# Fixed U columns as three 256-wide products, two more places for look-up operands, and counted gate rows one per step

## The chip, the cores and the metric

The kernel runs on one core of a Trainium2 chip. The metric is the device time of one execution in microseconds (us). TensorE multiplies matrices, VectorE and ScalarE work on rows, GpSimd does some row work and issues the DMAs whose rows are picked by index, SyncE's queue issues the plain loads. In the profile these are PE (PEld is its weight load), DVE, ACT, POOL and SP.

## The reference

One layer over 256 tokens of width 2048: retention and an RG-LRU side by side, cross attention over 256 memory tokens, then PEER, and a last norm. The change is in PEER:

```python
def peer_ffn(xn, w_q, sub_keys, u_tab, v_tab):
    q = (xt @ w_q).reshape(t, PEER_HEADS, 2, PEER_HALF)
    sub_scores = jnp.einsum('thcd,hckd->thck', q, sub_keys)
    vals, ids = lax.top_k(sub_scores, PEER_TOPK)
    cand = vals[:, :, 0, :, None] + vals[:, :, 1, None, :]
    top_sc, pos = lax.top_k(cand.reshape(t, PEER_HEADS, 256), PEER_TOPK)
    ...
    eid = (i1 * PEER_N_KEYS + i2)              # (t, 128) of 16384 experts
    gate = jax.nn.softmax(top_sc, axis=-1)
    ...
        act = gelu(einsum('td,tkd->tk', xb, u_tab[eid]))
        out = einsum('tk,tkd->td', gb * act, v_tab[eid])
```

All of it is float32.

## The kernel before

The 16384 experts are seen as 128 rows of 128. For 40 of these rows (`RD`), all 128 experts are computed for all 256 tokens, in five chunks of 8 rows: these are the fixed U columns and, later, chunks 0 to 4 of V. Of the other 88 rows' experts, the 32 groups that most tokens chose are gathered by a list (`dyn`, found by counting): four more chunks, 5 to 8, the gathered U and V columns. What is left over of a token's choices is taken token by token: 38 gathers of U for each half of the tokens (a dot product on VectorE, L1438) and 38 of V (an addition, L1446). All gathers are issued by GpSimd (L1431, L1215, L1263).

A product is kept exact to float32 by a split: the weights `raw` (128x1024, 512 KB) become `hi`, rounded on ScalarE (L133), and `lo`, the rest, on VectorE (L134); the activations `xn` stand as two halves of 256 columns, high and low. For a U column, `w_mms` (L136) does, for each of two halves of the weights, 8 products of `hi` with both halves of `xn` at once (512 wide, L143) and 8 of `lo` with the high half (256 wide, L145). Then `u_chunk` folds: ScalarE copies the right 256 columns of the sum (L1161), VectorE adds the left ones (L1162), ScalarE takes the gelu (L1163).

Beside the fixed U columns runs side work, in this order: `route` (the top-16 search, VectorE; for each half of the tokens it ends with three transposes `rT`, L835), `gbuild` (counting: for four tokens at a time, one-hot rows on VectorE, L1113, a product with the gates on GpSimd, L1114, gate products G and counts on TensorE, L1127 and L1130, copies on ScalarE, L1133 and L1134; after every 32 tokens ScalarE's queue writes the gates to DRAM, `gd` and `gt`, L1137 to L1140), then `side`: `choose` finds the 32 groups, and `look_up` marks for each token's choices whether their group was chosen. A look-up takes eight operands of 1 MB, loaded by `at_load` on GpSimd (L977) into four places: the tile of `h[1]` and three tiles `at1` to `at3`, which stand where gate tiles `gs` stood that the writes to DRAM still read. After that come `pick` (a max search), a sum over tokens (`off`, L1030) and the spilling of what does not fit (L1057, `fl` L1536). How the columns and the side work are mixed is set by a credit (`wv.pump` after each half column) and then by the scheduler, which orders each engine's queue; the order of the later part is written out (`run`).

`run` works through a list of steps: W (a plain tile of weights), D and R (halves of a gathered row of U and V), G (a tile of gates). At each step it splits the weights for step t+2 and issues loads for up to step t+8 into free places: `spots` for W and G (four `raw` tiles, and two halves of a `kept` tile, `lent`, in the V chunks), `rows_u`, and `rows_v` (L1342). The V chunks are taken in the order 0, 1, 2, 3, 5, 6, 7, 8, 4. The counted gates of chunks 5 to 8 are read back by `gate_rows` (L1290): four gathers of 128x256 in a row into one place of `spots`, twice for each chunk, during the V chunks 0 to 3. `gate_columns` (L1299) then multiplies four columns of the activations.

Of the kernel before, what the change touches and what calls it, by code (L numbers as in the profile page):

```python
# [9 lines left out]
F32 = mybir.dt.float32  # L10
F32R = mybir.dt.float32r
BF16 = mybir.dt.bfloat16
# [6 lines left out]
P = 128  # L19
# [66 lines left out]
def hybrid_layer_kernel(ctx: ExitStack, tc: tile.TileContext, a: dict, out: bass.AP, dbg=None):  # L86
# [50 lines left out]
    def w_mms(j, hi, lo, xt, pt):  # L137
        highs = [(0, 8 * j + k) for k in range(8)]
        lows = [(1, 8 * j + k) for k in range(8)]
        for part, kb in highs + lows if j == 0 else highs[:7] + lows + highs[7:]:  # L140
            ks = slice((kb - 8 * j) * P, (kb - 8 * j + 1) * P)
            if part == 0:
                PE.matmul(pt, hi[:, ks], xt[:, kb, :], start=(kb == 0), stop=(kb == KB - 1))  # L143
            else:
                PE.matmul(pt[:, :T], lo[:, ks], xt[:, kb, :T], start=False, stop=False)  # L145

    def whalf(j, src, xt, pt, raw=None):
        hi, lo = split(raw_tile(src) if raw is None else raw)
# [825 lines left out]

    def at_load(i):
        tt, c = divmod(i, 4)
        G.dma_start(ats[i % 4].bitcast(BF16), i1d[tt, 32 * c:32 * c + 32].rearrange("s t -> (s t)")[None, :].to_broadcast([P, 32 * P]))  # L977

    def look_up(tt):
        fl = gx["b"][:, 1920:2048]  # L980
# [23 lines left out]
    def compact():  # L1004
# [68 lines left out]
                                   op0=ALU.is_equal, op1=ALU.mult, accum_out=spl["g"][:, bs])  # L1073
            yield 0.6
        count_rest()
        ring.extend(ats[1:])

    tr = {}

    def side():  # L1080
        tr["t"] = rp.tile([P, P + 1], F32, tag="cand", name="tri")
        nc.sync.dma_start(tr["t"], a["tri"])
        wv.rate = RK
        for i in (1, 2, 3):
            ats.append(slot("ms", [P, D], f"at{i}"))
            at_load(i)
        yield from choose()
        yield from compact()
# [65 lines left out]
    def u_chunk(i, cols=8):  # L1154
        new_act(i)
        for c in range(cols):
            pt = mm("U") if i or c else pt0
            if i or c:
                wblock([a["U"][8 * i + c, j] for j in range(2)], xn, pt)
            t = tp.tile([P, T], F32, tag="fold", name="foldu", bufs=1)  # L1160
            A.copy(t, pt[:, T:])  # L1161
            V.tensor_tensor(t, pt[:, :T], t, op=ALU.add)  # L1162
            A.activation(acts[i][:, c, :], t, AF.Gelu_apprx_tanh)  # L1163

    acc = {}

# [116 lines left out]
    def prep_steps(i, gap=2):  # L1283
        box = []

        def gate(g, tt):
            av = acts[i][:, :, tt * P:(tt + 1) * P].rearrange("p c (b t) -> p c b t", t=GT)
            V.tensor_tensor(av, g.rearrange("p (b c t) -> p c b t", c=8, t=GT), av, op=ALU.mult)

        def gate_rows(b, q):  # L1290
            for n in range(4):
                k = 8 * (i - NCH) + 4 * q + n
                G.indirect_dma_start(b[:, T * n:T * n + T], None, gt_,
                                     bass.IndirectOffsetOnAxis(ap=dyn[:, k:k + 1], axis=0),
                                     bounds_check=NS - 1, oob_is_err=False)

        def gate_columns(g, q):
            av = acts[i][:, 4 * q:4 * q + 4]
            V.tensor_tensor(av, g.rearrange("p (c t) -> p c t", c=4), av, op=ALU.mult)  # L1299
# [12 lines left out]

        reads = []
        if ND <= i < NCH:
            n = T // GT // TT
            reads = [Step("G", lambda b, tt=tt: nc.sync.dma_start(
                b, gd[i - ND, :, n * tt:n * tt + n].rearrange("p b c t -> p (b c t)")),
                lambda g, tt=tt: gate(g, tt), 0) for tt in range(TT)]
        elif i >= NCH:
            reads = [Step("G", lambda b, q=q: gate_rows(b, q), lambda g, q=q: gate_columns(g, q), 0)  # L1320
                     for q in range(2)]
        post = {1: [(lambda: rounded(0), None)], 1 + gap: [(lambda: rounded(1), lambda: left(0))],
                1 + 2 * gap: [(None, lambda: left(1))]}
        return reads, {} if i in PLAIN else post
# [5 lines left out]
    ahs, spare = {}, {}  # L1330
    spots, rows_u, rows_v, lent = [], [], [], []

    def run(steps):
        raws, his, los, pts, later = {}, {}, {}, {}, {}
        queues = {k: [t for t, s in enumerate(steps) if s.kind in k and s.load] for k in ("WG", "D", "R")}
        free = {"WG": spots, "D": rows_u, "R": rows_v}

        def loads(t):
            for k, q in queues.items():
                while q and q[0] <= t + (4 if k == "R" else 0) and free[k]:  # L1340
                    t = q.pop(0)
                    raws[t] = free[k].pop(0)  # L1342
                    if k != "WG":
                        raws[t + 1] = raws[t]
                    steps[t].load(raws[t])

# [8 lines left out]
                    rows_u.append(raws[t])  # L1355

        def high(t):
            if t < len(steps) and steps[t].kind != "G" and not steps[t].plain:
                his[t] = ws.tile([P, 1024], F32R, tag="hi", name="hi", bufs=4)
                if steps[t].kind == "D":  # L1360
                    for n in range(2):
                        A.copy(his[t][:, 512 * n:512 * n + 512], pts[t][n])  # L1362
                else:
                    A.copy(his[t], part_of(t))  # L1364
# [4 lines left out]
        def low(t):  # L1369
            if t >= len(steps) or steps[t].plain:  # L1370
                return
            kind = steps[t].kind
            if kind == "G":
                steps[t].mms(raws[t])
            else:
                los[t] = ws.tile([P, 1024], F32R, tag="lo", name="lo", bufs=3)
# [6 lines left out]
                    V.tensor_tensor(los[t], part_of(t), his[t].bitcast(F32), op=ALU.subtract)  # L1383
            if kind in "WG":
                spots.append(raws[t])
            elif kind == "R" and steps[t].part:
# [15 lines left out]
        for t, step in enumerate(steps):  # L1402
# [5 lines left out]
            high(t + 3)  # L1408
            low(t + 2)
            loads(t + 8)  # L1410
            if step.plain:
                step.mms(raws[t])
                if step.part:
                    rows_v.append(raws[t])
                del raws[t]
            elif step.kind != "G":
# [6 lines left out]
            if step.kind != "G":  # L1423
# [252 lines left out]
    while "xn" not in done:  # L1676
        wv.pump(1.0)
    pt0 = mm("U")
    wblock([a["U"][0, 0], a["U"][0, 1]], xn, pt0)
    for b in (KB - 2, KB - 1):  # L1680
        sub_scores(b)
    pa.__exit__(None, None, None)
# [69 lines left out]
    for n, (i, nxt) in enumerate(zip(ORDER[:-1], ORDER[1:])):  # L1752
# [7 lines left out]
                attach(part[-1], {1: [(lambda m=m: given(m), None)]})  # L1760
        for k, g in enumerate(reads if nxt < NCH else []):
            part.insert(2 + 5 * k, g)
        if n < len(early_reads):
            for k, g in enumerate(early_reads[n]):
                part.insert(12 + 3 * k, g)
        steps += part
    with tc.manual_schedule(engines=ENGINES):
        run(steps)
# [95 lines left out]
```

## Time and profile before

| | |
|---|---|
| median of three runs | 2024.96 us |
| the three runs | 2024.9, 2024.96, 2029.99 us |
| the profiled execution | 2025.13 us, its span 2023.3 us |
| mean granted clock of TensorE | 0.974 |
| PE, DVE, ACT, POOL busy | 1897.9, 1518.9, 863.6, 508.4 us |
| HBM read, written | 503.24 MB, 21.30 MB (259 GB/s over the span) |
| U loads, V loads, to landing (median) | 3.8 us, 8.5 us |

The span is from the first to the last instruction of the profiled execution. Busy times of matmuls have modelled ends, so products that follow each other overlap in them; how close they follow is read from their starts. A wait is put down to what ended last before it. The fixed U columns run from 875 to 1259 us of the span, the gathered ones to 1514, the V chunks to 1952.

### The profile page before, as it was taken

To read this page: it belongs to the slowest core of one execution; us is meant where nothing else is said; L and a number is where in the kernel's file an instruction comes from. 1 tells how busy PE (TensorE), PEld (TensorE's weight loads), DVE (VectorE), ACT (ScalarE), POOL (GpSimd) and SP (SyncE) were. 2 spreads that over 40 slices of the span, in tenths; PEclk is the share of its full clock that TensorE was granted. 3 is DMA by queue.
4 is the path that set the end of the run, shared out by engine and by line. 5 is a ranking of instruction groups with operands and counts; after the bars stand their busy time and mean duration, and the time that the engine had idled before them with its cause. 6 is when DMAs were issued, how large, how long until landed. Compare 5 with 4: busy or idle time off the path is not lost.

```text
span 2023.3 us, 27282 instructions
## 1 busy us (share of the span) xinstructions
PE 1897.9 (94%) x10004; PEld 1556.1 (77%) x10004; DVE 1518.9 (75%) x2348; ACT 863.6 (43%) x1364; POOL 508.4 (25%) x371
## 2 busy tenths in 40 slices
PE   9999999999999999999898779999899799989798
PEld 8888888888889888888788767889787577455463
DVE  6868967754566557999978657899798797666667
ACT  6566444544555455554456523333343333020211
POOL 1200010000000000000045410555436556466524
PEclk9999999999999999999999889999899899999999
DMA  8775656566655457556458694998989799979983
GB/s 295 260 228 171 201 178 193 162 192 194 183 175 156 144 180 296 171 168 208 150 142 163 158 297 142 397 403 289 381 319 378 275 365 397 349 286 380 388 342 123
DMA packets 203242, 499.84 MB, mean 247 GB/s; under 512 B 106760, under 2 KB 113032, under 8 KB 174856
## 3 DMA queue, kind: packets, MB, share of 16 engines
q1 hardware_dynamic: 72288, 254.23, 38.0%
q0 software_dynamic: 36240, 228.29, 29.0%
q10 hardware_dynamic: 94576, 15.54, 4.4%
q8 instruction: 79, 1.29, 0.3%
q14 instruction: 59, 0.48, 0.1%
HBM read 503.24 MB, written 21.30 MB: 259 GB/s over the span
## 4 chain that ended last, share of the span: by engine, by line
PE 55%; DMA 15%; DVE 11%; issue 10%; POOL 5%; ACT 2%; ACTq 1%; POOLq 0%; SPq 0%; DVEq 0%
PE wb L143 10%; PE xc L185 6%; PE xc L186 6%; PE xc L188 6%; PE wb L145 5%; PE U L143 5%; DMA at<-in_Us_dram,idx 4%; PE acc L1613 3%; DVE lo L134 3%; PE U L145 2%; DMA gt<-gs 2%; DMA raw<-in_V_dram 2%; POOL at L1431 2%; DMA kept<-in_Vs_dram,dyn 1%; PE G L1127 1%
## 5 line engine op out<-in xcount | busy, mean ns | idle before, releaser
L134 DVE TENSOR_TENSOR lo<-raw,hi 128x1024 fp32r<-128x1024 f32 x364 | 448.7, 1235 | 206.9 <-PE xc L188 123.8
L133 ACT CAST hi<-raw 128x1024 fp32r<-128x1024 f32 x364 | 381.8, 1052 | 287.0 <-PE xc L186 173.0
L143 PE MATMUL U<-xn,hi 128*128 128x512 f32 x1152 | 314.3, 409 | 0.0
L143 PEld LDWEIGHTS U<-xn,hi 128*128 128x128 f32 x1152 | 213.6, 195 | 36.8
L1438 DVE SCALAR_TENSOR_TENSOR junk<-at,h 128x2048 bf16<-128x2048 f32 x72 | 164.6, 2286 | 21.2 <-DMA at<-in_Us_dram,idx 21.1
L145 PEld LDWEIGHTS U<-xn,lo 128*128 128x128 f32 x1152 | 157.9, 192 | 23.5 <-DVE lo L134 12.3
L145 PE MATMUL U<-xn,lo 128*128 128x256 f32 x1152 | 163.2, 284 | 9.3 <-DVE lo L134 9.3
L1446 DVE SCALAR_TENSOR_TENSOR hh<-at,coef,hh 128x2048 f32<-128x2048 f32 x49 | 116.0, 2368 | 50.1 <-DMA at<-in_Vs_dram,idx 49.4
L1364 ACT CAST hi<-kept 128x1024 fp32r<-128x1024 f32 x52 | 53.9, 1051 | 198.7 <-DMA kept<-in_Vs_dram,dyn 111.2
L781 POOL DMA_DIRECT2D hn<-h x2 | 1.1, 565 | 509.0 <-DVE h L779 509.0
L143 PE MATMUL wb<-hT,hi 128*128 128x512 f32 x448 | 116.9, 396 | 0.0
L1431 POOL DMA_INDIRECT at<-in_Us_dram,idx x72 | 82.4, 1144 | 125.2 <-DVE junk L1438 102.0
L1197 PE MATMUL acc<-kept,kept 128*128 128x512 f32 x256 | 110.2, 592 | 0.0
L1114 POOL TENSOR_TENSOR kept<-kept 128x512 f32<-128x512 bf16 x64 | 77.5, 1218 | 122.9 <-DVE kept L1113 88.9
L1197 PEld LDWEIGHTS acc<-kept,kept 128*128 128x128 f32 x256 | 48.6, 190 | 60.5 <-issue 60.0
L143 PEld LDWEIGHTS wb<-hT,hi 128*128 128x128 f32 x448 | 80.6, 189 | 13.9
L1113 DVE TENSOR_TENSOR kept<-kept,kept 128x512 bf16<-128x512 bf16 x128 | 69.7, 591 | 28.0 <-POOL kept L1114 15.0
L1127 PE MATMUL G<-kept,kept 128*128 128x128 f32 x512 | 73.1, 295 | 18.5 <-POOL kept L1114 9.6
L1431 POOL DMA_INDIRECT at<-in_Vs_dram,idx x49 | 73.4, 1498 | 66.3 <-DVE hh L1446 28.8
L143 PE MATMUL wb<-xT,hi 128*128 128x512 f32 x352 | 88.9, 393 | 0.0
L1127 PEld LDWEIGHTS G<-kept,kept 128*128 128x128 f32 x512 | 67.2, 207 | 22.4 <-POOL kept L1114 13.1
L1380 DVE TENSOR_TENSOR lo<-uT,hi 128x512 fp32r<-128x512 f32 x128 | 82.0, 684 | 2.4 <-ACT hi L1362 1.4
(492 smaller groups left out, 4133.2 us busy)
## 6 DMA issues: line engine op xcount, KB each, us to landing
raw<-in_U_dram SPq DMA_DIRECT2D x80, 512.0 KB, 3.8
raw<-in_w_qkv_dram SPq DMA_DIRECT2D x48, 512.0 KB, 4.2
raw<-in_w_xyg_dram SPq DMA_DIRECT2D x44, 512.0 KB, 4.1
raw<-in_V_dram SPq DMA_DIRECT2D x44, 512.0 KB, 8.5
raw<-in_w_xk_dram SPq DMA_DIRECT2D x32, 512.0 KB, 3.6
raw<-in_w_xv_dram SPq DMA_DIRECT2D x32, 512.0 KB, 3.5
raw<-in_w_out_dram SPq DMA_DIRECT2D x32, 512.0 KB, 3.5
raw<-in_w_xq_dram SPq DMA_DIRECT2D x32, 512.0 KB, 3.5
```

The costliest lines, as they stand in the source:

```text
L133: A.copy(hi, raw)
L134: V.tensor_tensor(lo, raw, hi.bitcast(F32), op=ALU.subtract)
L143: PE.matmul(pt, hi[:, ks], xt[:, kb, :], start=(kb == 0), stop=(kb == KB - 1))
L145: PE.matmul(pt[:, :T], lo[:, ks], xt[:, kb, :T], start=False, stop=False)
L185: PE.matmul(pt, xh, hi[:, w], start=(n == 0 and k == 0), stop=False)
L186: PE.matmul(pt, xl, hi[:, w], start=False, stop=False)
L188: PE.matmul(pt, xh, lo[:, w], start=False, stop=(n == 7 and k == 1))
L1127: PE.matmul(pt.rearrange("p (c t) -> p c t", t=4)[:, :, j], o1[:, j], og[:, j], start=True, stop=True)
L1197: PE.matmul(acc[dc][tt], av[:, c, tt * P:(tt + 1) * P], row[:, dc * 512:(dc + 1) * 512], start=False, stop=False)
L1431: G.indirect_dma_start(dst, None, src, bass.IndirectOffsetOnAxis(ap=ix, axis=0), bounds_check=n - 1, oob_is_err=False)
L1438: V.scalar_tensor_tensor(junk, gat, 1.0, h[0], op0=ALU.mult, op1=ALU.mult, accum_out=coef[tt][:, k:k + 1])
L1446: V.scalar_tensor_tensor(hh[tt], gat, coef[tt][:, k:k + 1], hh[tt], op0=ALU.mult, op1=ALU.add)
```

## The change

1. The fixed U columns use `u_block`: for each half of the weights, 8 products of `hi` with the high half of `xn`, 8 of `hi` with its low half, and 8 of `lo` with the high half, all 256 wide and all into the same 256 columns. The gelu reads the sum directly; the copy and the addition are gone. The gathered U columns stay as they were.
2. Look-up operands have six places: `gx["a"]` and `gx["d"]`, which counting used for its one-hot rows, come after `at1` to `at3`, and five loads are issued at the start of `side`. Afterwards only the three `at` tiles go to the token gathers.
3. The counted gates of chunks 5 to 8 are read by a step of a new kind, K, which takes a whole row buffer of `rows_v` (2048 wide) instead of two places of `spots`. Its load puts eight gathers on a list, `pending`, and `run` issues one of them at each step, up to 12 steps ahead. One `gate_columns` multiplies all eight columns. The four K steps stand in V chunks 1, 2 and 3 of the order (one, two and one); before, two G steps stood in each of 0 to 3.

```diff
+    def u_block(srcs, pt):
+        for j, src in enumerate(srcs):
+            hi, lo = split(raw_tile(src))
+            for part in range(3):
+                for k in range(8):
+                    kb = 8 * j + k
+                    x = xn[:, kb, T:] if part == 1 else xn[:, kb, :T]
+                    PE.matmul(pt[:, :T], (lo if part == 2 else hi)[:, k * P:(k + 1) * P], x,
+                              start=(part == 0 and kb == 0), stop=(part == 2 and kb == KB - 1))
+            wv.pump(wv.rate)
...
-                wblock([a["U"][8 * i + c, j] for j in range(2)], xn, pt)
-            t = tp.tile([P, T], F32, tag="fold", name="foldu", bufs=1)
-            A.copy(t, pt[:, T:])
-            V.tensor_tensor(t, pt[:, :T], t, op=ALU.add)
-            A.activation(acts[i][:, c, :], t, AF.Gelu_apprx_tanh)
+                u_block([a["U"][8 * i + c, j] for j in range(2)], pt)
+            A.activation(acts[i][:, c, :], pt[:, :T], AF.Gelu_apprx_tanh)
...
-        G.dma_start(ats[i % 4].bitcast(BF16), ...)
+        G.dma_start(ats[i % 6].bitcast(BF16), ...)
...
-        for i in (1, 2, 3):
-            ats.append(slot("ms", [P, D], f"at{i}"))
+        ats.extend(slot("ms", [P, D], f"at{i}") for i in (1, 2, 3))
+        ats.extend((gx["a"], gx["d"]))
+        for i in range(1, 6):
             at_load(i)
...
-            reads = [Step("G", lambda b, q=q: gate_rows(b, q), lambda g, q=q: gate_columns(g, q), 0)
-                     for q in range(2)]
+            reads = [Step("K", lambda b: pending.extend((b, n, gate_row) for n in range(8)), gate_columns, 0)]
...
             loads(t + 8)
+            if pending:
+                b, n, f = pending.pop(0)
+                f(b, n)
...
-        if n < len(early_reads):
-            for k, g in enumerate(early_reads[n]):
-                part.insert(12 + 3 * k, g)
+        for m, k in ((0, 12),) if n == 1 else ((1, 6), (2, 15)) if n == 2 else ((3, 8),) if n == 3 else ():
+            part.insert(k, early_reads[m][0])
```

GpSimd's queue at the end of counting and the look-up, before (L1114 is counting's product, `i1d` the operands, `h` and `at` their places, `row` a gathered U column):

```order
L977 DMA at_10568<-i1d 128x4096
L1114 TENSOR_TENSOR kept_7748<-kept_7750 128x512 x2
L977 DMA h_4236<-i1d 128x4096
L977 DMA at_10566<-i1d 128x4096
L977 DMA at_10568<-i1d 128x4096
L977 DMA at_10570<-i1d 128x4096
L1215 DMA row_11592<-in_Us_dram,dyn 128x2048
L1215 DMA row_11593<-in_Us_dram,dyn 128x2048
L977 DMA at_10570<-i1d 128x4096
```

and now (`kept` are the two new places):

```order
L988 DMA at_10952<-i1d 128x4096
L1126 TENSOR_TENSOR kept_7764<-kept_7766 128x512 x2
L988 DMA kept_7766<-i1d 128x4096
L988 DMA kept_7763<-i1d 128x4096
L988 DMA h_4236<-i1d 128x4096
L988 DMA at_10951<-i1d 128x4096
L1224 DMA row_12112<-in_Us_dram,dyn 128x2048
L988 DMA at_10953<-i1d 128x4096
L1224 DMA row_12113<-in_Us_dram,dyn 128x2048
```

Loads 4 and 5 now stand ahead of the second use of `h` and `at1`; the load into the third place (`at_10953`), of operand 3, is the last one, and no load stands behind it.

TensorE's queue at the end of the side work, from a spill product to the first gathered column (`uT`), before:

```order
L1057 MATMUL spill<-ct,own 128x1 x2
L1536 MATMUL fl<-flag,ones 128x2
L143 MATMUL U<-xn,hi 128x512
L145 MATMUL U<-xn,lo 128x256 x8
L143 MATMUL U<-xn,hi 128x512 x9
L145 MATMUL U<-xn,lo 128x256 x8
L143 MATMUL U<-xn,hi 128x512 x7
L145 MATMUL U<-xn,lo 128x256 x8
L143 MATMUL U<-xn,hi 128x512 x9
L145 MATMUL U<-xn,lo 128x256 x8
L143 MATMUL U<-xn,hi 128x512 x7
L145 MATMUL U<-xn,lo 128x256 x8
```

and now:

```order
L1068 MATMUL spill<-ct,own 128x1 x2
L1548 MATMUL fl<-flag,ones 128x2
L154 MATMUL U<-xn,hi 128x256 x5
L154 MATMUL U<-xn,lo 128x256 x8
L154 MATMUL U<-xn,hi 128x256 x16
L154 MATMUL U<-xn,lo 128x256 x8
L1361 MATMUL uT<-ident,row_12112 128x128 x16
```

2.31 columns stood behind the last side product, 0.77 stand there now. Counted along the same queue, the second trio of `rT` stands behind 21.0 columns (20.4 before), the first counting product behind 23.0 (20.5), the look-ups of operands 0 to 2 behind 31.5 (29.9), that of operand 3 behind 33.5 (32.0), and `off` behind 38.0 (36.5).

GpSimd's queue in the V chunks, where gate rows stand among the token gathers, before:

```order
L1431 DMA at_10566<-in_Us_dram,idx 128x2048
L1293 DMA kept_7751<-gt,dyn 128x256 x4
L1431 DMA at_10568<-in_Us_dram,idx 128x2048
L1431 DMA h_4236<-in_Us_dram,idx 128x2048
L1293 DMA raw<-gt,dyn 128x256 x4
L1431 DMA at_10570<-in_Us_dram,idx 128x2048
```

and now:

```order
L1443 DMA at_10953<-in_Us_dram,idx 128x2048
L1301 DMA kept_7768<-gt,dyn 128x256 x2
L1443 DMA at_10951<-in_Us_dram,idx 128x2048
L1301 DMA kept_7768<-gt,dyn 128x256 x2
L1443 DMA at_10952<-in_Vs_dram,idx 128x2048
L1301 DMA kept_7768<-gt,dyn 128x256
L1443 DMA h_4236<-in_Vs_dram,idx 128x2048
```

Four rows in one piece became one or two between token gathers, and their target is a row buffer (`kept_7768`) in place of `raw` and half of a lent tile.

More of the change, by code (lines that the diff above doesn't have):

```diff
@@ L976, in at_load @@
         tt, c = divmod(i, 4)
-        G.dma_start(ats[i % 4].bitcast(BF16), i1d[tt, 32 * c:32 * c + 32].rearrange("s t -> (s t)")[None, :].to_broadcast([P, 32 * P]))
+        G.dma_start(ats[i % 6].bitcast(BF16), i1d[tt, 32 * c:32 * c + 32].rearrange("s t -> (s t)")[None, :].to_broadcast([P, 32 * P]))
     def look_up(tt):
@@ L1075, in compact @@
         count_rest()
-        ring.extend(ats[1:])
+        ring.extend(ats[1:4])
     tr = {}
@@ L1288, in gate, with gate_row, gate_columns @@
             V.tensor_tensor(av, g.rearrange("p (b c t) -> p c b t", c=8, t=GT), av, op=ALU.mult)
[L1290 to L1299, printed above, removed]
+        def gate_row(b, n):
+            k = 8 * (i - NCH) + n
+            G.indirect_dma_start(b[:, T * n:T * n + T], None, gt_,
+                                 bass.IndirectOffsetOnAxis(ap=dyn[:, k:k + 1], axis=0),
+                                 bounds_check=NS - 1, oob_is_err=False)
+        def gate_columns(g):
+            V.tensor_tensor(acts[i], g.rearrange("p (c t) -> p c t", c=8), acts[i], op=ALU.mult)
         def rounded(k):
@@ L1331, in hybrid_layer_kernel @@
     spots, rows_u, rows_v, lent = [], [], [], []
+    pending = []
     def run(steps):
         raws, his, los, pts, later = {}, {}, {}, {}, {}
-        queues = {k: [t for t, s in enumerate(steps) if s.kind in k and s.load] for k in ("WG", "D", "R")}
-        free = {"WG": spots, "D": rows_u, "R": rows_v}
+        queues = {k: [t for t, s in enumerate(steps) if s.kind in k and s.load] for k in ("WG", "D", "K", "R")}
+        free = {"WG": spots, "D": rows_u, "K": rows_v, "R": rows_v}
         def loads(t):
             for k, q in queues.items():
-                while q and q[0] <= t + (4 if k == "R" else 0) and free[k]:
+                while q and q[0] <= t + (4 if k in "KR" else 0) and free[k]:
                     t = q.pop(0)
                     raws[t] = free[k].pop(0)
-                    if k != "WG":
+                    if k in "DR":
                         raws[t + 1] = raws[t]
@@ L1357, in high @@
         def high(t):
-            if t < len(steps) and steps[t].kind != "G" and not steps[t].plain:
+            if t < len(steps) and steps[t].kind not in "GK" and not steps[t].plain:
                 his[t] = ws.tile([P, 1024], F32R, tag="hi", name="hi", bufs=4)
@@ L1372, in low @@
             kind = steps[t].kind
-            if kind == "G":
+            if kind in "GK":
+                assert all(p[0] is not raws[t] for p in pending)
                 steps[t].mms(raws[t])
@@ L1385, in low @@
                 spots.append(raws[t])
-            elif kind == "R" and steps[t].part:
+            elif kind == "K" or kind == "R" and steps[t].part:
                 rows_v.append(raws[t])
@@ L1415, in run @@
                 del raws[t]
-            elif step.kind != "G":
+            elif step.kind not in "GK":
                 step.mms(his.pop(t), los.pop(t))
@@ L1422, in run @@
                 later.setdefault(t + n, []).extend(fs)
-            if step.kind != "G":
+            if step.kind not in "GK":
                 wv.pump(step.rate)
@@ L1678, in hybrid_layer_kernel @@
     pt0 = mm("U")
-    wblock([a["U"][0, 0], a["U"][0, 1]], xn, pt0)
+    u_block([a["U"][0, 0], a["U"][0, 1]], pt0)
     for b in (KB - 2, KB - 1):
```

## The prediction

> **What bounds the kernel now.** I read the page first, then the table of stretches, then the waits of TensorE in the two stretches that the change touches, and last the chain and the timelines around single waits. The table has, for each stretch, its length, the busy time of each engine with its instructions, the granted clock, the share of the DMA engines and GB/s.
>
> ```profile
> core 0: us, PE busy (x) PEld busy (x) DVE busy (x) ACT busy (x) POOL busy (x), PEclk, DMA share, GB/s
> 905.00:1002.00 97.00, 88.51 (x495) 75.94 (x494) 97.00 (x288) 45.55 (x70) 3.12 (x3) 0.98 0.57 177
> 1002.00:1165.00 163.00, 140.45 (x1052) 128.85 (x1051) 120.24 (x207) 95.59 (x228) 75.98 (x64) 0.94 0.68 155
> 1165.00:1199.00 34.00, 20.47 (x205) 17.34 (x205) 16.95 (x30) 8.46 (x12) 4.24 (x6) 0.84 0.97 299
> 1199.00:1245.00 46.00, 42.50 (x349) 36.76 (x347) 40.43 (x171) 15.52 (x23) 2.62 (x2) 0.89 0.57 202
> ...
> 1259.00:1514.00 255.00, 243.09 (x1535) 215.43 (x1534) 222.43 (x287) 94.49 (x204) 126.30 (x93) 0.97 0.92 353
> 1514.00:1725.00 211.00, 182.97 (x759) 146.81 (x759) 174.56 (x142) 72.45 (x75) 121.20 (x72) 0.94 0.92 355
> 1725.00:1905.00 180.00, 169.71 (x506) 95.67 (x505) 123.51 (x68) 26.97 (x27) 108.28 (x66) 0.99 0.89 344
> ```
>
> The fixed U columns run from 875 to 1259, four stages one behind the other: routing (VectorE is full, 97.00 of 97), counting, the look-up, and picking with spilling. No engine is full in the last three, so waits set their length. The V chunks run from 1514 to 1725 with the DMA engines at 0.92. The gathered U columns between them (1259 to 1514) are not touched. TensorE's own waits in the fixed U columns:
>
> ```profile
> PE G L1127 <- POOL kept L1114: 9.6, 2, 6.3
> PE U L145 <- DVE lo L134: 9.3, 7, 4.4
> PE G L1127 <- ACT kept L1116: 8.9, 10, 3.4
> PE look L988 <- DVE at L984: 8.9, 1, 8.9
> PE rT L835 <- DVE rt L910: 5.3, 1, 5.3
> ```
>
> These five are 42.0 us of 384. The U columns are what fills TensorE while the side work runs; a microsecond is won only where a column moves from the end of the stretch into such a hole.
>
> **The three 256-wide products.** One column in full flow, from the chain (start, length, what, count):
>
> ```profile
> 892.26 2.07 PE U L143 x9
> 894.33 0.95 PE U L145 x8
> 895.28 1.61 PE U L143 x7
> 896.89 0.95 PE U L145 x8
> 897.85 1.16 PE U L143 x5
> ```
>
> A column takes 897.85 - 892.26 = 5.59 us: 16 products of 512 and 16 of 256. Eight 256-wide ones, each with weights of its own, take 0.95, so 48 take 6 x 0.95 = 5.70. That is +0.11 a column, +4.4 for 40 columns, if TensorE had no holes at all; I count it inside the column times below.
>
> On the same place a rule speaks against the change. The Trainium skill, "TensorE: Matmul & The Clock Gate", section "The mechanism", says that a weight load overlaps matmuls in flight only when the row groups differ; here all use all 128 rows, and there are 640 more loads. The trace disagrees: eight products with eight loads take 0.95, 0.119 each, while the page has L145's weight load at 192 ns, so the loads overlap. The term is +4.4 by the row; what the rule would give is the last rival.
>
> The fold goes: a copy on ScalarE and an addition on VectorE for each column.
>
> ```profile
> L1162 DVE TENSOR_TENSOR foldu<-U,foldu 128x256 f32<-128x256 f32 x17 | 7.0, 410 | 0.0
> ...
> L1161 ACT COPY foldu<-U 128x256 f32<-128x256 f32 x40 | 14.8, 371 | 21.0 <-PE U L143 20.9
> ```
>
> The first row is of the routing stretch alone: 17 additions, 7.0 us, on the engine that is full there. The end of routing, and where the first counting products came:
>
> ```profile
> 1000.15 0.31 DVE rt L910
> 1000.50 0.48 PE rT L835
> ...
> 1002.69 1.58 PE G L1127 x8
> ...
> 1018.37 0.23 PE U L143
> ```
>
> VectorE ends routing at 1000.5; without 7.0 us of additions, and with some 1.3 us more of weight splitting for 0.6 column, at about 995. TensorE's queue now has 21 columns ahead of the second routing transpose (20.4 before). The product at 892.26 is the last of column 3, so three columns were done at 892.5; they take 0.3 more now, and 18 others 18 x 5.70 = 102.6: 995.4. The 5.3 us wait goes. Two more columns stand before the first counting product, so column 23 ends at about 1007.5, the transposes included; before it ended at 1018.6, with 2.8 us of counting done on the way. TensorE is 8 us ahead in columns, and these 8 us are not needed later.
>
> **Counting (1002 to 1165).** It starts 5 us later now, holds 8.5 columns instead of 9.3 (-4.6), and loses some nine copies on ScalarE and additions on VectorE (3.4 and 3.8 us on engines that are not full). I leave its end where it was: between 5 later (nothing of this helps) and 15 sooner (most of TensorE's 22.5 us idle in it goes, since columns now alternate evenly with counting).
>
> **Two more places.** Look-up operands 4 and 5 had to wait for a place that an earlier look-up gave back. What ended last was another wait:
>
> ```profile
> 1192.11 0.53 POOL L977 DMA_DIRECT2D at<-i1d  x1 [19.50 <-DMA gt<-gs]
> ...
> 1197.67 1.42 DVE L984 TENSOR_SCALAR at<-at,tri 128x2048 bf16<-128x2048 bf16 x2 [10.61 <-DMA at<-i1d]
> ...
> 1198.48 0.59 PE L988 MATMUL look<-words,at 128*128 128x11 bf16 x16 [8.91 <-DVE at L984]
> ...
> DVE h L984 <- DMA h<-i1d: 4.7, 1, 4.7
> ```
>
> The load into the third place waits until the last gate write has landed, at 1192; VectorE and TensorE wait for it. That place has the same source of waiting afterwards, and GpSimd's queue now has it behind loads 4 to 7. So the early loads take away the 4.7 us wait of the last row, but the wait for the third place takes it back: 0, between -4.7 and +4, the latter if two 1 MB loads more slow that write (DMA share 0.97 there).
>
> **Picking and spilling, and the end.** From the third place on, VectorE is busy 40.43 of 46; 5.7 additions of 0.41 leave it: -2.4. The last side product and the first gathered column:
>
> ```profile
> 1244.56 0.36 PE L1536 MATMUL fl<-flag,ones 128*128 128x2 f32 x2
> ...
> 1258.60 1.64 PE L1353 MATMUL uT<-ident,row 128*128 128x128 f32 x13 [0.98 <-DVE foldu L1162]
> ```
>
> Between them stood 2.31 columns, 14.0 us with the last fold; now 0.77, 0.77 x 5.70 = 4.4. That is -9.6, the same 8 us gained at the front and the fold that TensorE waited for. Sum of the U columns: -2.4 - 9.6 = -12.
>
> **Gate rows one per step.** TensorE, then GpSimd, SyncE's queue and VectorE in the V chunks, and one gate row's issue:
>
> ```profile
> PE acc L1178 <- DVE lo L1383: 23.1, 9, 6.0
> PE acc L1175 <- ACT hi L1364: 5.0, 1, 5.0
> ...
> POOL kept L1293 <- DVE lo L1383: 10.9, 2, 10.3
> POOL raw L1293 <- DVE lo L1383: 9.0, 3, 7.4
> ...
> SPq L1275 <- DVE kept L1299: 10.5, 6, 4.0
> SPq L1275 <- DMA raw<-gt,dyn: 6.9, 5, 3.0
> ...
> DVE kept L1299 <- DMA kept<-gt,dyn: 10.6, 2, 9.8
> DVE kept L1299 <- DMA raw<-gt,dyn: 6.8, 4, 3.5
> ...
> L1293 POOL DMA_INDIRECT raw<-gt,dyn x20 | 37.5, 1875 | 14.1 <-DVE lo L1383 9.0 <-issue 4.6 <-DMA kept<-gt,dyn 0.3
> ...
> 1689.28 13.21 DMA raw<-gt,dyn x2
> ```
>
> TensorE idles 28.1 us. Gate rows shared the six V places: GpSimd stood 19.9 us for a place with token gathers queued behind, SyncE held V loads 17.4 us until a gate tile was done, VectorE stood 17.4 us for gate rows. In row buffers these three have no cause: the buffer is given back a stage earlier, and V loads keep six places. The 32 row issues (1.9 us each) stay on GpSimd, busy 121 of 211, spread one to a step; nothing else is added to it, and SyncE issues the same loads. The two half multiplications become one, of the same size.
>
> What it is worth is bounded by DMA: 0.92 of 211 us is 194 us of transfers that remain, so at most 17 go, and TensorE's 28.1 cannot all go. Below, a gain fails if V loads were late for bandwidth alone (0), and a late gate row would stop VectorE's queue, with the split of a later V tile behind it (a loss of 6, if two rows land 8 us late). I take the middle of 0 and 17, since the stalls in view are about half places and half landing: -9. Later, the third V row buffer is free two gathers later; its look-ahead is twelve steps: 0, at most +2.
>
> **Sum.** The profiled execution took 2025.13 (span 2023.3 and 1.8 around it), 0.2 above the median of 2024.96: 2025.1 - 12 - 9 = 2004.
>
> **The rivals.** (1) Bandwidth takes the V gain: 2025 - 12 = 2013. For it speaks 0.92, against it the 1.9 us rows that held places. (2) Counting shortens by 15 as well, the last gate write lands sooner, and V gains 12: 2025 - 12 - 15 - 12 = 1986. For it speaks the even alternation, against it that ScalarE's gate writes stay. (3) Nothing shows: counting ends 5 later, the write stretches by 4, V gains nothing: 2025 - 12 + 9 = 2022. (4) Slower, by the gate rows: each of four multiplications waits on VectorE for its last row, which took 13.21 to land at 1689, and V tiles behind it are split late. With no lead at all that is 4 x 13 = 52 us; with a lead of a step and a half (4 us) it is 36, the V gain of 9 falls away, and TensorE loses about 22: 2025 - 12 + 22 = 2035. It decides from 4.6 us a multiplication (18 us, which cancels the U gain and 0.3%). Against it: the last of eight rows goes out about four steps of 2.7 us ahead. (5) Weight loads don't overlap: 640 x 0.192 = 123 us more, 2148 less the other gains, 2127; the 0.95 row is against it. The Trainium skill's rule above is this one.
>
> **How the numbers follow.** The forecast, 1995 to 2012, has 0.50; (1) 0.16, (2) 0.14, (3) 0.09, (4) 0.10, (5) 0.01. The range reaches to (2) and to (3): 1986 to 2022. Faster by over 0.3% (6 us, about what a measurement of this kernel can tell from no change) is the forecast with (1) and (2), and a little of (3): 0.81; within: most of (3), 0.08; slower: (4) and (5), 0.11.
>
> **What would show it.** U columns of 48 products at 5.7 us; no fold on either engine; the second routing transpose without wait; the first gathered column at about 1247; the third place still waiting for the gate write. In the V chunks no wait of GpSimd or SyncE for gate tiles, TensorE idle under 20 us, and the stretch near 202 us with a DMA share above 0.95. Wrong would make it: VectorE standing at the gate multiplication, or a gate write that lands later than 1192.

## The result and the profile after

The changed kernel took 1997.76 us (median of 4 runs, 1993.28 to 2009.42; a fifth execution on record took 2002.18) beside 2027.47 us of the kernel before (4 runs, 2024.9 to 2033.72): a ratio of 0.986, 95% interval 0.9818 to 0.9902. The forecast was 2004, with 1986 to 2022 as its range. That was a fall of 21 us; measured were 29.7 here, and 23.5 and 23.1 in the two groups below that ran both kernels on one chip. The profiled execution of the changed kernel is the slowest of its runs, 2009.42 us. Two more profiled executions of it, below, took 1996.0 and 2010.5.

The stretches of this execution, with each engine's busy time and instructions, the granted clock, the DMA share and GB/s:

```profile
core 0: us, PE busy (x) PEld busy (x) DVE busy (x) ACT busy (x) POOL busy (x), PEclk, DMA share, GB/s
905.00:1002.00 97.00, 92.46 (x745) 89.79 (x744) 96.86 (x284) 41.95 (x55) 3.91 (x4) 1.00 0.60 181
1002.00:1161.00 159.00, 143.60 (x1257) 140.82 (x1256) 106.79 (x182) 94.98 (x221) 70.52 (x65) 0.97 0.76 172
1161.00:1200.00 39.00, 20.27 (x245) 19.62 (x245) 19.73 (x38) 8.03 (x11) 4.52 (x6) 0.85 0.95 293
1200.00:1242.00 42.00, 42.00 (x447) 41.81 (x445) 37.65 (x162) 11.62 (x16) 1.00 (x1) 0.88 0.58 180
...
1506.00:1715.00 209.00, 185.48 (x768) 147.49 (x767) 174.37 (x139) 72.54 (x75) 136.31 (x72) 0.95 0.94 361
```

Picking (1200 to 1242) now has TensorE full. The look-up (1161 to 1200) holds as little work as it did and takes no less time: TensorE is busy 20.27 us of 39, where it was 20.47 of 34. TensorE's waits in the fixed U columns (who waits for whom: us in total, times, longest) say why:

```profile
PE look L999 <- DVE at L995: 14.9, 1, 14.9
PE cnt L1142 <- DVE kept L1125: 10.0, 6, 1.8
PE U L154 <- DVE lo L134: 6.7, 10, 2.3
PE G L1139 <- POOL kept L1126: 4.5, 1, 4.5
...
PE G L1139 <- ACT kept L1128: 0.9, 1, 0.9
```

The third look-up place is still the last to be ready. GpSimd's load into it, and TensorE's first gathered column:

```profile
1193.23 0.57 POOL L988 DMA_DIRECT2D at<-i1d  x1 [22.96 <-DMA gt<-gs]
```

```profile
1241.64 0.36 PE L1548 MATMUL fl<-flag,ones 128*128 128x2 f32 x2
...
1247.02 3.71 PE L1361 MATMUL uT<-ident,row 128*128 128x128 f32 x32 [0.47 <-ACT kept L1172]
```

In the plain V chunks, the waits of TensorE, of GpSimd and of VectorE (only the rows on gates, weight halves and token rows):

```profile
PE acc L1187 <- DVE lo L1392: 18.6, 8, 8.6
PE acc L1184 <- ACT hi L1372: 4.6, 2, 4.4
...
POOL kept L1301 <- DVE kept L1306: 1.6, 1, 1.6
...
DVE kept L1306 <- DMA kept<-gt,dyn: 7.5, 1, 7.5
DVE hh L1458 <- DMA h<-in_Vs_dram,idx: 7.1, 2, 4.1
DVE hh L1458 <- DMA at<-in_Vs_dram,idx: 6.5, 3, 2.9
DVE junk L1450 <- DMA at<-in_Us_dram,idx: 1.1, 1, 1.1
```

For a place to put gate rows in, GpSimd waited 19.9 us and now waits 1.6. VectorE's 17.4 for gate rows are 7.5, all in one wait, and SyncE's queue has no row for gathered gate tiles any more. But VectorE now waits 14.7 us for token rows, where before it waited 3.8:

```profile
DVE junk L1438 <- DMA at<-in_Us_dram,idx: 1.9, 1, 1.9
...
DVE hh L1446 <- DMA at<-in_Vs_dram,idx: 1.5, 1, 1.5
...
DVE hh L1446 <- DMA h<-in_Vs_dram,idx: 0.4, 1, 0.4
```

So on VectorE the one wait was exchanged for the other, and TensorE's waits in the stretch fell only from 28.1 us to 23.2.

The stages of all profiled executions, in us, read from first starts on TensorE: the first fixed U column, the first gathered column (`uT`), the first V product, the first product of a gathered gate-weighted row (`acc<-kept,kept`), the first of the last V chunk (`acc<-last,kept`).

| execution | fixed U | gathered U | V chunks, plain | V chunks, gathered | both V |
|---|---|---|---|---|---|
| before | 384.0 | 255.6 | 214.6 | 223.4 | 438.0 |
| changed | 373.5 | 258.9 | 209.5 | 221.0 | 430.5 |
| changed, first group | 373.4 | 254.4 | 201.9 | 219.1 | 421.0 |
| changed, third group | 376.1 | 255.8 | 209.5 | 220.5 | 430.0 |
| products alone | 375.5 | 257.8 | 220.2 | 220.3 | 440.5 |
| places alone | 383.7 | 257.0 | 213.3 | 220.0 | 433.3 |
| gate rows alone | 383.7 | 254.1 | 203.9 | 218.2 | 422.1 |
| without the places | 369.0 | 256.3 | 201.8 | 218.6 | 420.4 |
| five places, second group | 364.1 | 256.2 | 203.7 | 221.3 | 425.0 |
| five places, third group | 364.0 | 255.2 | 203.6 | 220.2 | 423.8 |
| four places | 368.5 | 255.8 | 203.7 | 218.5 | 422.2 |
| rows at once | 374.6 | 256.7 | 209.0 | 220.6 | 429.6 |
| no gate reads | 370.5 | 257.4 | 193.3 | 219.5 | 412.8 |
| narrow with fold | 383.3 | 256.6 | 203.7 | 216.6 | 420.3 |

One profile of one kernel moves by some 3 us in the fixed U columns and by 10 in V, so a single row bears only larger differences.

### The profile page after: what moved, and what is told of

It is laid out like the page before. It is cut to its first block, busy times and chain, and to the rows that moved or that the text cites. A ratio compares the mean times of both kernels' runs of the same rounds, so it can differ in the third digit from the quotient of the medians.

```text
span 2007.6 us, 28472 instructions
## 1 busy us (share of the span) xinstructions
PE 1897.4 (95%) x10644; PEld 1586.3 (79%) x10644; DVE 1498.8 (75%) x2304; ACT 851.2 (42%) x1324; POOL 521.5 (26%) x371
## 4 chain that ended last, share of the span: by engine, by line
PE 53%; DMA 19%; DVE 14%; issue 9%; POOL 4%; ACT 1%; POOLq 0%; ACTq 0%; SPq 0%; DVEq 0%
PE wb L143 7%; PE xc L196 7%; PE xc L197 7%; PE xc L199 7%; PE U L154 6%; DMA at<-in_Us_dram,idx 4%; PE wb L145 4%; DVE lo L134 4%; PE acc L1625 3%; DMA at<-in_Vs_dram,idx 3%; DMA gt<-gs 2%; DMA h<-in_Vs_dram,idx 2%; PE G L1139 2%; POOL at L1443 2%; PE U L143 1%
## 5 line engine op out<-in xcount | busy, mean ns | idle before, releaser
L1450 DVE SCALAR_TENSOR_TENSOR junk<-at,h 128x2048 bf16<-128x2048 f32 x72 | 164.5, 2284 | 22.8 <-DMA at<-in_Us_dram,idx 16.1
L154 PE MATMUL U<-xn,hi 128*128 128x256 f32 x1280 | 176.8, 289 | 1.5 <-ACT hi L133 1.5
L154 PEld LDWEIGHTS U<-xn,hi 128*128 128x128 f32 x1280 | 164.3, 196 | 1.7 <-ACT hi L133 1.7
L143 PE MATMUL U<-xn,hi 128*128 128x512 f32 x512 | 140.3, 407 | 0.0
L1372 ACT CAST hi<-kept 128x1024 fp32r<-128x1024 f32 x52 | 53.9, 1050 | 199.9 <-DMA kept<-in_Vs_dram,dyn 58.6
L143 PEld LDWEIGHTS U<-xn,hi 128*128 128x128 f32 x512 | 93.0, 192 | 15.4
L1126 POOL TENSOR_TENSOR kept<-kept 128x512 f32<-128x512 bf16 x64 | 72.0, 1133 | 127.3 <-DVE kept L1125 90.3
L154 PE MATMUL U<-xn,lo 128*128 128x256 f32 x640 | 93.6, 289 | 6.9 <-DVE lo L134 6.7
L1443 POOL DMA_INDIRECT at<-in_Vs_dram,idx x49 | 87.1, 1777 | 47.4 <-DVE hh L1458 20.5
L154 PEld LDWEIGHTS U<-xn,lo 128*128 128x128 f32 x640 | 84.1, 195 | 9.9 <-DVE lo L134 9.5
L1125 DVE TENSOR_TENSOR kept<-kept,kept 128x512 bf16<-128x512 bf16 x128 | 63.4, 542 | 32.8 <-PE cnt L1142 21.8
```

What stands on the lines that cost most here:

```text
L154: PE.matmul(pt[:, :T], (lo if part == 2 else hi)[:, k * P:(k + 1) * P], x, start=(part == 0 and kb == 0), stop=(part == 2 and kb == KB - 1))
L1443: G.indirect_dma_start(dst, None, src, bass.IndirectOffsetOnAxis(ap=ix, axis=0), bounds_check=n - 1, oob_is_err=False)
L1450: V.scalar_tensor_tensor(junk, gat, 1.0, h[0], op0=ALU.mult, op1=ALU.mult, accum_out=coef[tt][:, k:k + 1])
```

## First group: the parts one by one

Four kernels on one chip, beside 2022.48 us of the kernel before (16 runs).

**Products alone.** `u_block` in place of `wblock`, the fold gone, nothing else changed.

```diff
-                wblock([a["U"][8 * i + c, j] for j in range(2)], xn, pt)
...
+                u_block([a["U"][8 * i + c, j] for j in range(2)], pt)
+            A.activation(acts[i][:, c, :], pt[:, :T], AF.Gelu_apprx_tanh)
```

> The kernel before with the three 256-wide products alone. Theory A (columns move from the end of the U stretch into TensorE's holes): the first gathered column (uT) starts about 11 us earlier than before (1247 against 1258.6), a column in full flow takes 5.7 us, the V chunks are as before: 2014, 0.995 of before. Rival B (the early look-up loads did it, the products alone cost 4.4 us): uT not earlier than 1257, 2025 or more.

Measured: 2009.41 us, ratio 0.9939 (0.9919 to 0.9958). The fixed U columns took 375.5 instead of 384.0, and the first gathered column came at 1250.39, 8 us earlier where 11 were expected.

**Places alone.** Six places, five early loads, old products, old gate steps.

```diff
-        G.dma_start(ats[i % 4].bitcast(BF16), ...)
+        G.dma_start(ats[i % 6].bitcast(BF16), ...)
```

> The kernel before with the two more look-up places alone. Theory A: operand 3's load still waits for the last gate write and TensorE waits for it, so uT starts within 3 us of 1258.6 and the time is that of before, ratio 0.998 to 1.002. Rival B: the loads of operands 4 and 5 were on the path, uT is 5 to 10 us earlier, ratio 0.996.

Measured: 2028.68 us, ratio 1.0025 (1.0006 to 1.0045). The fixed U columns are no shorter (383.7), and V, 4.7 us shorter in this profile, stays within what profiles of one kernel differ by. The load into the third place waits for the gate write as before, and goes out later (1192.11 before), by GpSimd's timeline:

```profile
1196.62 0.57 POOL L977 DMA_DIRECT2D at<-i1d  x1 [20.41 <-DMA gt<-gs]
```

**Gate rows alone.** The K steps, with wide products and four places.

```diff
...
+            reads = [Step("K", lambda b: pending.extend((b, n, gate_row) for n in range(8)), gate_columns, 0)]
```

> The kernel before with the gate rows in row buffers alone. Theory A: U stretch as before, the V chunks 7 to 10 us shorter, GpSimd and SyncE no longer wait for gate tiles: ratio 0.996. Rival B (V is bound by bandwidth, and the profiled 7 us were chance): V chunks within 2 us, ratio 1.000. Rival C: more than 15 us gained here, since the unprofiled executions of the changed kernel were some 12 us shorter than the profiled one.

Measured: 2010.16 us, ratio 0.9948 (0.9932 to 0.9965). The plain V chunks took 203.9 us and moved their bytes at a higher rate than before (0.92, 355 GB/s), as its row in the table of stretches shows:

```profile
1515.00:1718.00 203.00, 183.37 (x766) 145.84 (x765) 174.64 (x138) 72.39 (x75) 132.80 (x73) 0.97 0.95 371
```

**The whole change.**

> The changed kernel once more, beside the parts on the same chip. Theory A: the parts add up, ratio 0.988 to 0.992, uT at about 1247 and the last V product some 8 to 15 us closer to uT than before. Rival: the parts don't add, and the change is worth more than their sum.

Measured: 1998.99 us, ratio 0.9893 (0.9874 to 0.9912). The three ratios multiply to 0.9912, the upper end of its interval: products and gate rows make the gain in about equal parts, and the places give none.

## Second group: the wait for the gate write, and the gate rows

Beside 2023.94 us of the kernel before (11 runs).

**Five places.** The third place, which stands where a late gate tile stood, is left out; the token gathers get it afterwards as before.

```diff
-        G.dma_start(ats[i % 6].bitcast(BF16), ...)
+        G.dma_start(ats[i % 5].bitcast(BF16), ...)
...
-        ats.extend(slot("ms", [P, D], f"at{i}") for i in (1, 2, 3))
+        ats.extend(slot("ms", [P, D], f"at{i}") for i in (1, 2))
```

> The changed kernel with five look-up places instead of six: the third gate-tile place, which waits for the last write of the gates to DRAM, holds no operand any more; operand 3 goes into the first of the two former counting tiles. Theory A (the wait for that write is what ends last in the look-up): TensorE's stop of 14.9 us before the look-up products shrinks to 6 us or less, the first gathered column comes near 1238 instead of 1247, and the kernel takes 8 to 12 us less than the changed one (1987 to 1991 beside 1999). Rival B (a stop that goes is replaced: VectorE, which picks afterwards, has its own chain): the wait gets short but the first gathered column stays within 3 us of 1247, and the time within 3 us. Rival C (the two places cost through GpSimd's queue or through their loads, not through the wait): no change of either.

Measured: 1992.86 us, ratio 0.9842 (0.9824 to 0.9861). The last gate write landed as late as ever, 32.8 us after its issue, but no operand waits for it now. The first gathered column came at 1238.84, and of the stop in the look-up these of TensorE's waits are left:

```profile
PE look L999 <- DVE at L995: 2.0, 1, 2.0
PE look L999 <- DVE h L995: 1.5, 1, 1.5
```

**Four places: `h[1]`, `at1` and the two former counting tiles.**

```diff
-        G.dma_start(ats[i % 6].bitcast(BF16), ...)
+        G.dma_start(ats[i % 4].bitcast(BF16), ...)
...
+        ats.append(slot("ms", [P, D], "at1"))
+        ats.extend((gx["a"], gx["d"]))
```

> The changed kernel with four look-up places: the tile of h[1], the first gate-tile place and the two former counting tiles. None of them waits for the last two writes of the gates, but operands 4 and 5 wait until an earlier look-up gives a place back, as before the change. Theory A: as with five places or better, first gathered column 1236 to 1240 and 8 to 12 us less than the changed kernel, since two 1 MB loads fewer run beside the write. Rival B (a place that is given back late ends last now): the stop moves to a later look-up operand, first gathered column 1243 or later, within 4 us of the changed kernel.

Measured: 1992.31 us, ratio 0.9844 (0.9821 to 0.9867). The first gathered column came at 1241.99. Among TensorE's waits a different one of 8.2 us appears, for `words`, the look-up's other input, and not for an operand:

```profile
PE look L999 <- DVE words L970: 8.2, 1, 8.2
...
PE look L999 <- DVE kept L995: 1.8, 2, 1.6
```

Both kernels say that which places are used counts for more than how many: without the one that waits for the gate write, four take the same time as five (their fixed U columns 368.5 and 364.1).

**Gate rows at once.**

```diff
-            if pending:
+            while pending:
                 b, n, f = pending.pop(0)
```

> The changed kernel, but the eight gate rows of a chunk are issued in a row as soon as a row buffer is free, instead of one at each step. Theory A (what the change wins in V comes from the places: gate rows no longer hold the places of V loads): the V stretch stays within 3 us of the changed kernel, and so does the time. Rival B (the spacing counts: eight rows of 1.9 us each, 15 us, stand on GpSimd ahead of the token gathers): VectorE waits for token rows after each block, TensorE for the split behind them, and the kernel takes 5 to 12 us more than the changed one.

Measured: 2004.99 us, ratio 0.9907 (0.9883 to 0.9932), against 0.9893 and 0.9888 of the changed kernel, with overlapping intervals. VectorE's wait for gate rows is gone, and it waits longer for token rows: 20.4 us in all (12.9, 6.7 and 0.8) beside 14.7 in the changed kernel's profile (6.5, 1.1 and 7.1). Its waits, in us in total, times, longest:

```profile
DVE hh L1458 <- DMA at<-in_Vs_dram,idx: 12.9, 2, 7.2
DVE junk L1450 <- DMA at<-in_Us_dram,idx: 6.7, 2, 5.7
```

One wait has been exchanged for the other. That the spacing itself gains is not shown. That the row buffers gain without it is likely: products alone and places alone multiply to 0.9964, above this kernel's interval, though they ran on another chip.

**No gate reads.** The 32 gathers are left out, and the activations of chunks 5 to 8 are multiplied by what the buffer holds, so that the result is not the layer's.

```diff
-            reads = [Step("K", lambda b: pending.extend(...), gate_columns, 0)]
+            reads = [Step("K", lambda b: None, gate_columns, 0)]
```

> The changed kernel without reading the counted gates back: the 32 gathers are left out, 4 MB of 128 KB rows, and the activations of chunks 5 to 8 are multiplied by what the row buffer holds. Theory A (the DMA engines are full in the V chunks, so only bytes and descriptors count there): the V stretch, 202 us, falls by what 4 MB take at 355 GB/s, 12 us, and the kernel takes 8 to 12 us less. Rival B (TensorE and VectorE set the stretch once the places are free): it falls by 4 us or less.

Measured: 1992.12 us, ratio 0.9842 (0.9824 to 0.986). The plain V chunks took 193.3 us; their row in the table of stretches:

```profile
1502.00:1695.00 193.00, 182.17 (x768) 145.80 (x768) 173.89 (x139) 72.24 (x75) 81.68 (x40) 0.97 0.94 368
```

Beside it, the changed kernel in the first group:

```profile
1502.00:1704.00 202.00, 182.07 (x770) 145.25 (x769) 173.61 (x138) 72.51 (x75) 129.43 (x72) 0.97 0.96 370
```

The rate stays at 368 to 370 GB/s, and 4 MB less take 9 us less (11 at that rate). TensorE is busy 182 us in both. This would fit a stretch that is held by its bytes, with TensorE 11 us behind as the next bound, but it is not shown: without the reads VectorE's one wait for a gate row (7.3 us in the first group's profile) is gone too, and TensorE's waits fell from 19.8 us to 10.7, by the same 9 us. The rows at once took that wait away and kept the bytes, but brought other waits, so no run here separates the two.

## Third group: places within the change, and the fold

Beside 2024.58 us of the kernel before (11 runs).

> The changed kernel, as the base of this group on one chip: ratio 0.987 to 0.991 to the kernel before, first gathered column at 1247 to 1249.

Measured: 2001.45 us, ratio 0.9888 (0.9864 to 0.9911); the first gathered column came at 1251.7, later than expected, with the start 2 us later too.

**Without the two places**, otherwise the changed kernel (`ats[i % 4]`, three early loads):

> The changed kernel with the four look-up places of before (products and gate rows only). Theory A (the two early loads cost: they lie beside the last gate writes and delay their landing, for which the third place waits): the write lands 3 to 5 us sooner, the first gathered column comes at 1243 to 1246, and the kernel takes 3 to 6 us less than the changed one. Rival B (the places are worth nothing either way, and the 0.25% of the run with the places alone is an accident of that run): first gathered column and time within 2 us of the changed kernel. Rival C (beside the narrow products the operands are needed sooner, so the places help): 3 us more.

Measured: 1996.16 us, ratio 0.9871 (0.9851 to 0.9891). The median is 5.3 us lower, but the intervals overlap. Its wait for the operand is 8.5 us instead of 14.7, and the last gate write landed 23.8 us after its issue instead of 32.9, in time for a load at 1187 instead of 1197, by GpSimd's timeline (the row names ScalarE's split, since that ended last before it):

```profile
1187.23 1.04 POOL L988 DMA_DIRECT2D at<-i1d  x2 [18.18 <-ACT hi L133]
```

The fixed U columns with four old places took 369.0 here and 375.5 in the products alone, with six and the same products 370.5 to 376.1. So a cost of two early loads of some 5 us is likely (two comparisons, 1.0025 alone and this one) but not settled.

**Five places again.** The edit of the second group.

> The changed kernel with five look-up places, of which none waits for the last gate write, now beside the changed kernel on one chip. Theory A (the wait is worth its idle time): 6 to 10 us less than the changed kernel, first gathered column at 1238 to 1240. Rival B: within 3 us.

Measured: 1993.29 us, ratio 0.9846 (0.9826 to 0.9867); 8.2 us below the changed kernel on the same chip, and together with four places the fastest version here that computes the layer.

**Narrow products, fold kept.** The products of the low half of `xn` go into the right 256 columns; the first and last product of a column stay 512 wide.

```diff
...
+                    PE.matmul(pt[:, T:] if part == 1 else pt[:, :T], (lo if part == 2 else hi)[:, k * P:(k + 1) * P], x,
+                              start=False, stop=False)
...
+            A.copy(t, pt[:, T:])
+            V.tensor_tensor(t, pt[:, :T], t, op=ALU.add)
+            A.activation(acts[i][:, c, :], t, AF.Gelu_apprx_tanh)
```

> The changed kernel with narrow products but with the fold kept: the products of the low half of the activations go into the right 256 columns of the sum again (the first and last product of a column are 512 wide), and ScalarE's copy and VectorE's addition are back. Theory A (the fold's departure makes the gain of the U columns, the narrow shape itself costs a little): first gathered column at 1257 to 1264 and 10 to 15 us more than the changed kernel. Rival B (the shape and the order of the products make the gain, because the low halves are needed later in a column): first gathered column at 1250 or sooner, time within 3 us of the changed kernel.

Measured: 2010.78 us, ratio 0.994 (0.9924 to 0.9956), 9.3 us above the changed kernel. The fixed U columns took 383.3 us, as with wide products; TensorE's timeline has the first gathered column at 1257.37:

```profile
1257.37 3.71 PE L1371 MATMUL uT<-ident,row 128*128 128x128 f32 x32 [0.97 <-DVE foldu L1181]
```

So the narrow shape neither gains nor costs anything that shows, and the fold's departure is the gain of the U columns. Where it arises, a table of the U columns' own instructions from 1050 to 1150, in the middle of counting, tells in part. Before:

```profile
1050.00:1150.00 100.00, 24.39 (x124) 19.16 (x124) 2.48 (x6) 2.34 (x6) 0.97 0.72 144
```

Changed:

```profile
1050.00:1150.00 100.00, 37.56 (x259) 33.83 (x258) 0.00 (x0) 2.34 (x6) 0.98 0.84 173
```

Narrow with fold:

```profile
1050.00:1150.00 100.00, 26.70 (x180) 24.04 (x180) 2.48 (x6) 2.38 (x6) 0.97 0.77 151
```

At 32, 48 and 46 products a column these are 3.9, 5.4 and 3.9 columns in the same 100 us. The window overstates the difference, since fewer of counting's gate products stand in it in the changed kernel (360 beside 390 and 383). Better are two instants that the two narrow kernels have in common. At 1003.9, when the second routing transposes run, the changed kernel had done 21.00 columns and the one with the fold 20.33; at their last gate products, at 1160.1 and 1160.5, they had done 30.67 and 29.09. So some 0.7 of a column arises during routing, where VectorE is full, and 0.9 in counting. TensorE's waits in counting, with the fold:

```profile
PE G L1146 <- ACT kept L1135: 6.7, 8, 3.1
PE G L1146 <- POOL kept L1133: 6.4, 1, 6.4
PE cnt L1149 <- DVE kept L1132: 3.8, 6, 1.3
```

The wait for ScalarE's counting copies, 8.9 us before and 0.9 after, is back at 6.7 with the fold. But the wait for VectorE's one-hot rows, 3.9 before and 10.0 after, is back too, at 3.8, and the three waits add up to 22.4 us before, 15.4 after and 16.9 with the fold. So no single one of these rows measures what the fold costs in counting. Whether ScalarE's copy or VectorE's addition does it was not tried apart.

## Why the prediction was right, and which steps were not

**U columns, -12 forecast, -10.5 measured** (384.0 to 373.5). The forecast of 1247 for the first gathered column came out at 1247.02. Its terms: up to the third place's load it was 0 and is +2.2 (that load 1.1 later, the start 1.1 earlier); from there to the last flag -2.4 and -4.0 (48.41 us instead of 52.45); from the flag to the first gathered column -9.6 and -8.7 (5.38 us instead of 14.04). The last term was read from the order of TensorE's queue, 0.77 columns in place of 2.31, and came out; but the path that was to pay for it did not.

**The step that failed: the second routing transpose at 995, and the 8 us won ahead of counting.** VectorE did end its part at 995 (its timeline in the changed kernel):

```profile
994.77 0.28 DVE L839 TENSOR_TENSOR rr<-rt 128x128 f32<-128x128 f32 x1
```

But TensorE reached the transpose only at 1003.91, without a wait (its timeline):

```profile
883.12 2.08 PE L154 MATMUL U<-xn,hi 128*128 128x256 f32 x16
...
888.88 2.08 PE L154 MATMUL U<-xn,hi 128*128 128x256 f32 x16
...
953.48 1.22 PE L154 MATMUL U<-xn,lo 128*128 128x256 f32 x8 [1.62 <-DVE lo L134]
...
1003.91 0.27 PE L846 MATMUL rT<-ident,rt 128*128 128x128 f32 x1
...
1015.75 1.05 PE L1139 MATMUL G<-kept,kept 128*128 128x128 f32 x8
```

Undisturbed, a column takes 888.88 - 883.12 = 5.76 (5.70 forecast). The three first columns ended at 891.76, and the 18 after them took 112 us, 6.2 each: I took the undisturbed pace for all, on a stretch where VectorE, which makes the low halves, is full and the low half of the weights comes late again and again. TensorE's waits for that half from 890 to 1004 are nine, of 4.4 us in all. The first counting product came at 1015.75, behind 23.0 columns, and not at 1007.5. The kernel before was as far at 1018.6, with 2.8 us of counting done by then: TensorE had no lead.

The 8 us were won in counting, which I had left as it was. From the second transposes to the last gate product it took 156 us with 9.7 columns in it (1003.91 to 1160.1). By the forecast's terms the same work stood in 168 us (995.4 to 1163.2, the old end), and before it took 163 us with 8.7 columns (1000.5 to 1163.2). TensorE's waits in it are 15.4 us instead of 22.4. I priced the folds' nine copies and additions in counting at nothing because their engines aren't full there; the run with the fold puts them at 0.9 of a column. So the total of -12 came out near by luck: the gain ahead of counting was put too high and the gain in counting too low, by about as much.

**Two more places, 0 forecast (-4.7 to +4).** The third place does take the gain back, as forecast; the measured cost leans to the upper end. The prediction named a gate write that lands after 1192 as a sign against it, and this came, by a little: the write landed at 1192.7 in the profile beside the forecast, and between 1192.4 and 1196.9 in all seven with six places.

**Gate rows, -9 forecast.** The three profiles with old gate steps have V at 438.0, 440.5 and 433.3, mean 437.3; the nine with K steps and one row a step, the gate reads in place, have a mean of 423.9: -13.4. The forecast is of the plain chunks alone, where the means are 216.0 and 204.6: -11.4, inside 0 to 17 and a little more than the -9 of the sum. Together with the -10.5 of the U columns the -13.4 makes -23.9, near the 23.5 and 23.1 of the two groups. In the profile put beside the forecast it was only -7.5, with +3.3 in the gathered U columns, which nothing touches. TensorE idles 23.2 us there (under 20 forecast), and the stretch is 209.5 (202 forecast); in the first group's execution both come out, 19.8 and 201.9, with a DMA share of 0.96. The bound that I drew at 194, the time in which the DMA engines were busy, is 0.96 of 202 in that execution, so the transfers remained and the rest went. The run without gate reads moves 4 MB less, so its 193.3 is no test of that bound.

**The rivals.** (1), bandwidth takes the V gain: no, the rate rose from 355 to 370 GB/s. (2), counting ends 15 sooner: no, its last gate product came 3 us sooner, with one more column done in it. (3), nothing shows: no. (4), gate rows late on VectorE, which the prediction named as the other sign against it: it happens, at one of the four multiplications, and in all nine profiles with one row a step (6.2 to 7.9 us). The second block's eighth row went out 1.1 us before VectorE was free for the multiplication at 1617.36 (the end of the splits before it), and TensorE stood behind the next split (the timelines of GpSimd, VectorE and TensorE):

```profile
1616.27 1.97 POOL L1301 DMA_INDIRECT kept<-gt,dyn  x1 [0.30 <-issue]
```

```profile
1624.86 2.29 DVE L1306 TENSOR_TENSOR kept<-kept,kept 128x2048 f32<-128x2048 f32 x1 [7.50 <-DMA kept<-gt,dyn]
```

```profile
1630.60 1.65 PE L1187 MATMUL acc<-lo,xe 128*128 128x512 f32 x3 [8.55 <-DVE lo L1392]
```

Its row buffer came free only with the first block's multiplication, 1585.42 to 1587.7, and at one row a step the lead was used up. It is one wait of 7.5, not four of 4.6, so the gain is not lost. What it takes of the gain isn't shown: with the rows at once the wait is gone, and others stand in its place. (5), weight loads that don't overlap: no. The 48 narrow products of the column above, each with a weight load, take 5.76 us, 0.120 each, while one load lasts 0.196 by its group row:

```profile
L154 PEld LDWEIGHTS U<-xn,hi 128*128 128x128 f32 x1280 | 164.3, 196 | 1.7 <-ACT hi L133 1.7
```

The Trainium skill's rule ("TensorE: Matmul & The Clock Gate", section "The mechanism"), by which a load overlaps only products of other row groups, doesn't hold for these full-height products; the measurement decides.

## What to carry to other kernels

Adding a place to a ring helps only if the place that comes free last is no longer on the path: look for the place with the late releaser and take it out, as five places did for 8 us beside six. Work on an engine that isn't full can still cost where another engine waits for it: the fold, priced at nothing in counting, was worth 0.9 of a column there, which the busy shares didn't tell, and a wait that goes may come back under another engine's name, so add up all of them. And a stage is not predicted by the pace of an undisturbed stretch when the engine that feeds it is full there.

## What the runs showed of the hardware that was not expected

A write of the gates to DRAM in short rows lands far later than its issue. The 16 writes and the gathers that read them back took, in the changed kernel, from 4.6 to 30.2 us, half of them above 7.3, by the row on these tiles:

```profile
DMA to landing us min/median/max: 4.6/7.3/30.2
```

The longest is the last write, for which the third place waits. It took 22.8 to 26.9 us in the four profiles with the four old places (the kernel before, products alone, gate rows alone, without the places). In the seven with six places, where two more loads of 1 MB are issued about its time, it took 28.5 to 32.9, with wide products and with narrow ones; with five places it took 28.7 and 32.8, with the other four 38.8. That the loads beside it delay it is likely by this, and not shown apart from the other differences in order.

With the same instructions, executions of the changed kernel differ by 9 us in V (421.0, 430.0, 430.5), at a mean rate of 370 and 361 GB/s; what sets which of them occurs stays open.
